# Up projection of a decoder layer: the halo kept in the first token half of four of seven parts; the two column halves of the first token tile of w_out no longer ordered one behind the other

## The chip, the cores and the metric

The kernel runs on one core of one Trainium2 chip. The metric is the device time of one execution in microseconds (us). Engines by the profile's names: PE is TensorE (matmuls; PEld its weight loads), DVE VectorE, ACT ScalarE, POOL GpSimd, SP SyncE, whose queue issues most DMAs.

## The reference

One layer over 16 meta tokens and 1024 tokens of width 1024. The part that matters here is its last third:

```python
mixed = jax.nn.sigmoid(g_attn) * y_attn + jax.nn.sigmoid(g_conv) * y_conv
h = layer_norm(DEEPNORM_ALPHA * h + mixed @ w_out, ln1_g, ln1_b)
up = causal_dwconv(h @ ffn_w_up, ffn_dw, ffn_dw_b)     # 3 taps, 2 x 2816 channels
u, g = jnp.split(up, 2, axis=-1)
f = (jax.nn.gelu(g, approximate=False) * u) @ ffn_w_down
return layer_norm(DEEPNORM_ALPHA * h + f, ln2_g, ln2_b)   # the meta tokens are dropped
```

The convolution has three taps and looks back, so each channel of a token needs the up projection of the two tokens before it too: the halo.

## The kernel before

All matrix products work on float32 split into a high and a low part, and add three products: high times high, high times low, low times high.

**Projection to `mixed` and w_out.** The last group of the projections (`ps_p`, L1173) is followed by `out_rows` (L1330 on), which multiplies `mixed` by w_out one tile of 128 tokens at a time, in the order 3, -1, 7, 2, 6, 0, 4, 1, 5. Tile -1 is the two tokens of the halo (the edge rows, L1358, matmuls of 32 rows). A tile has two column halves of 512; each is a PSUM buffer `ps_w` (three in turn under the tag `mm`) and 24 matmuls: eight blocks k of w_out rows, each with L340, L343 and L344 of `product`. Blocks 4 and 5 lie in RX and RW, 0 to 3 in OA, 6 and 7 in the two buffers `w`, and are split by a ScalarE cast (L300) and a VectorE subtraction (L303). `behind` gives `product` a matmul that its first one is to come after in program order; `after` puts such an order on two instructions without a semaphore. VectorE adds the residual (L1346; it is loaded from `h0d`), takes the statistics and normalizes (L1372); `turn` transposes the tile and ScalarE writes it with gain and offset to FA (L1395).

**Up projection.** It is one level of Strassen's scheme in Winograd's form: the tokens make two halves h, the 1024 inputs two halves kk, the output channels two halves, and seven products ("parts") of half size replace eight. The token side of the parts is `B11, B21, BT2, BT1, BT3, BT4, B22`: `bsub` forms the sums (`form_t2`, `form_t3`, `form_t4`) and `bsplit` splits each into `row(sub, q, 0)` and `row(sub, q, 1)`. Each half of 512 tokens is in turn cut into `sub` 0 (256 tokens, with the halo of two in front: 258 columns) and `sub` 1 (256). In `sub` 0 of each part the high operand has 260 columns: the low parts of the two halo columns, the high parts of the same two, and 256 more.

There are 22 chunks c of 128 + 128 output channels. In each, `prod` runs the parts in the order B11, B21, BT2, BT4, BT1, BT3, B22, and each part's `sub` 0 and then its `sub` 1, 12 matmuls each (L1597), into the PSUM tiles X (`px`), Z (`pz`), V4 (`pw`) and Y (`py`). In `sub` 0 the terms go by the kind of product (`j` in 0, 2, 1), since only two kinds hold the halo; in `sub` 1 they go by block k. Between the parts ScalarE copies X and Y out (L1609) and VectorE adds and subtracts them (L1605) to c11, c21 (first token half), c12 and c22 (second). `conv_ffn` first adds the two halo columns' low sums to their high ones (two activations of one column, L1521), then does the three taps. `w_ahead(9)` keeps the split weights of nine parts ready. Chunk 0 is run in two passes, `sub` 1 first.

**What sets the order.** A list scheduler with a timeline of its own orders each engine's instructions by `rank`, by dependences and by `after`; `line` pins VectorE's sums of the token side into one sequence. The down projection (L1742) follows.

Of the kernel before, what the change touches and what calls it, by code (L numbers as in the profile page):

```python
# [23 lines left out]
F = mybir.dt.float32  # L24
# [5 lines left out]
P = 128  # L30
# [83 lines left out]
def tile_hybrid_layer(  # L114
# [1118 lines left out]
            [(OC, OC_UP + i * 2048, 0) for i in range(4)] + [(RHC, x + R_DN, 0) for x in (4096, 2048, 6144)]]  # L1233
    B11, B21, BT2, BT1, BT3, BT4, B22 = range(7)

    def bsum(sub, q, hl):
        r = row(sub, q, hl)
        return r[:, :, 2:260] if sub == 0 and not hl else r

    def row(sub, q, hl):  # L1240
# [6 lines left out]
    def bmat(sub, q, j, k):  # L1247

        if sub:
            return row(1, q, j % 2)[:, k]  # L1250
        return row(0, q, j % 2)[:, k, 0:(260, 256, 260)[j]]

    lined, high = [], []
# [15 lines left out]

    def bsplit(sub, q, src, cs=slice(None)):  # L1270
        with rank(RK_SUMS):
            src = wide(src)[:, :, cs]
            hi = bsum(sub, q, 0)[:, :, cs]
            ins = nc.scalar.copy(hi, src)
            if (sub, q) in ((0, BT2), (0, BT4), (0, BT1), (0, BT3)):
                if high:
                    after(ins, high[-1])
                high.append(ins)
            n = src.shape[2]
            a = cs.start or 0  # L1280
            x = 2 if sub == 0 and a == 0 else 0
            a -= 2 if sub == 0 and a else 0
            lo = bsum(sub, q, 1)[:, :, a:a + n - x]
            line(nc.vector.tensor_tensor(lo, src[:, :, x:], f32(hi)[:, :, x:], OP.subtract))
            if x:
                line(nc.vector.tensor_tensor(row(0, q, 0)[:, :, 0:2], src[:, :, :2], f32(hi)[:, :, :2], OP.subtract))
# [28 lines left out]


    WO_ORDER = (4, 5, 0, 1, 2, 3, 6, 7)
    edge = const.tile([P, 2, KC, 2], F, name="edge")
    r_next, w_last = [1], []

    def out_rows(i, between=(), work=()):


        n, u = (P, 2 + i * P) if i >= 0 else (2, 0)
        if n == P:
            o = r_next[0] % 2 * 1024
            r_next[0] += 1
            whole = RT[:, o:o + 1024]
            load(whole, h0d[u:u + n, :])
        else:  # L1330
            whole = OB[:, 2048:3072]
        r = whole[:n]
        order = WO_ORDER if i != 5 else (0, 1, 2, 3, 6, 7, 4, 5)
        turned = None
        st = small.tile([P, 2, 6], F, name="st")
        pin = line if i in (0, 4, 1, 5) else lambda ins: ins
        for half in range(2):
            hs = slice(half * 512, half * 512 + 512)
            ps = pat.tile([P, 512], F, name="ps_w", tag="mm", bufs=3)
            if n == P:  # L1340
                behind = turned or (w_last[-1] if w_last else None)
                last = product(ps, [(mixed(i, k, 0), mixed(i, k, 1), wo[k][0][:, hs], wo[k][1][:, hs])
                                    for k in order], behind)
                w_last.append(last)
                with rank(RK_TURN):
                    pin(nc.vector.tensor_tensor(r[:, hs], ps, r[:, hs], OP.add))  # L1346
                    pin(nc.vector.bn_stats(st[:, half], r[:, hs]))
                turned = None
                if len(between) > half:
                    turned = turn(*between[half], behind=[last])  # L1350
                if half == 0:
                    for f, *x in work:
                        f(*x)
                continue

            for k in range(KC):
                o = k % 4 * 32
                last = nc.tensor.matmul(ps[o:o + 32], pair[:, 2 * k:2 * k + 32], wo_raw[k][:, hs], start=k < 4,  # L1358
                                        stop=k >= 4)
                after(last, w_last[-1])  # L1360
                w_last.append(last)
            nc.scalar.copy(whole[:, hs], ps)
        if n < P:
            for j, src in enumerate((h0d[0:2, :], whole[32:34], whole[64:66], whole[96:98])):
                q = FA[:2, j % 2 * 1024:j % 2 * 1024 + 1024]
                load(q, src)
                nc.vector.tensor_tensor(r, r, q, OP.add)
        with rank(RK_TURN):
            (mu, rs), = ln_stats([(r, n)], half_stats=st if n == P else None)
            for a in (512, 0) if i == 5 else (None,):  # L1370
                x = r if a is None else r[:, a:a + 512]
                ins = pin(nc.vector.tensor_scalar(x, x, mu, rs, OP.subtract, OP.mult))  # L1372
        if n == P:
            load(h1d[u - 2:u - 2 + P, :], r)
        return whole, n, ins

    def turn(i, r, n, ins, banks=None, behind=None, upper=False):
        with rank(RK_TURN):
            for j, k0 in enumerate((4, 0) if upper else (0, 4)):
                ps = banks[j] if banks else pat.tile([P, 512], F, name="ps_h", tag="s", bufs=2)  # L1380
                for k in range(4):
                    ins = nc.tensor.transpose(ps[:, k * P:(k + 1) * P], r[:, (k0 + k) * P:(k0 + k + 1) * P], ident)
                    if behind:
                        after(ins, behind[-1])
                        behind.append(ins)
                for k in range(k0, k0 + 4):
                    src = ps[:, (k - k0) * P:(k - k0) * P + n]
                    if n < P:
                        dst = edge[:, 0, k]
# [5 lines left out]
                    nc.scalar.activation(dst, src, AF.Identity, bias=b1col(k), scale=g1col(k))  # L1395
                    if i == 3:
                        nc.scalar.activation(edge[:, 1, k], src[:, P - 2:P], AF.Identity, bias=b1col(k), scale=g1col(k))
        return behind[-1] if behind else None


# [68 lines left out]
            w_ahead(n)  # L1469

    def edges():
        for h in range(2):
            with rank(RK_TURN):
                nc.vector.tensor_copy(FA[:, h * 2064:h * 2064 + 2064].rearrange("p (k n) -> p k n", n=258)[:, :, 0:2],
                                      edge[:, h])

    ahead = []
    work = {0: [(split_of, 1, B11), (split_of, 1, B21), (split_of, 1, B22)],
# [36 lines left out]
    c11, c21, u2 = (FA[:, 4128 + i * CU:4128 + (i + 1) * CU] for i in range(3))  # L1515
    c12, c22, u13 = (RT[:, i * CU:(i + 1) * CU] for i in range(3))

    def conv_ffn(cc, o):
        t = ftmp()
        for i in range(2):  # L1520
            nc.scalar.activation(cc[:, 2 + i:3 + i], cc[:, 2 + i:3 + i], AF.Identity, bias=cc[:, i:i + 1], scale=1.0)  # L1521
# [52 lines left out]
    for c in range(FC):  # L1574
        V4, X, Z, Y = (pup.tile([P, 1024], F, name=n, tag=n) for n in ("pw", "px", "pz", "py"))
        passes = ((1,), (0,)) if c == 0 else ((0, 1),)
        for subs in passes:
# [4 lines left out]
            def at(t):  # L1582
                return t[:, 252 + a:252 + b]

            def prod(q, bank, first):
# [4 lines left out]
                    ah, al = w_ready[next(w_next)]  # L1590
                for sub in subs:
                    terms = [(k, j) for k in range(4) for j in range(3)]
                    if sub == 0:
                        terms = [(k, j) for j in (0, 2, 1) for k in range(4)]
                    for i, (k, j) in enumerate(terms):
                        o = bank[:, 512:768] if sub else bank[:, (252, 256, 252)[j]:512]
                        ins = nc.tensor.matmul(o, (ah, ah, al)[j][:, k * P:(k + 1) * P], bmat(sub, q, j, k),  # L1597
                                               start=first and i == 0, stop=i == 11, skip_group_check=not first)
                        if i == 0 and last_mm:
                            after(ins, last_mm[-1])  # L1600
# [14 lines left out]
                sums_load(c - 1 if c <= FH else c - 2)  # L1615
            tt(c11[:, a:b], at(Z), u13[:, a:b], OP.add)
            prod(BT2, X, False)
            copy(u2[:, a:b], at(X))
            if not last:
                turn(5, *last_rows, (V4, Z), last_mm, True)  # L1620
                for q in (B11, B21):
# [11 lines left out]
            copy(c22[:, a:b], at(Y))  # L1633
            prod(BT3, X, False)
            copy(u13[:, a:b], at(X))
            ins = tt(c22[:, a:b], c22[:, a:b], u13[:, a:b], OP.add)
# [4 lines left out]
            tt(c12[:, a:b], at(Y), u2[:, a:b], OP.add)  # L1641
            if last:
                f1 = conv_ffn(c22, c)
                f_out(c, 0, g0, conv_ffn(c21, c))
                f_out(c, 1, gelu(conv_ffn(c12, FC + c)), f1)
    up_stack.close()


# [247 lines left out]
```

## Time and profile before

| | us |
|---|---|
| median of 3 runs (1251.36 to 1253.63) | 1251.79 |
| profiled execution | 1251.86 |
| its span | 1250.1 |
| TensorE busy in the span | 1236.5 |
| VectorE busy | 1079.4 |
| ScalarE busy | 627.6 |

The granted clock is 0.999. The span runs from the first profiled instruction to the last; the 1.8 us beside it are the start and end of the execution. Rows in order of time have the start, the length, the engine, the line, the operation, the tiles (written <- read) and the shape, then the count; a bracket has the idle time of the engine ahead of it and what ended that. Ends of matmuls are modelled and overlap, so the spacing of starts is what TensorE really takes.

### The profile page before, as it was taken

Reading aid. Unit: us, or ns where it says so; the run is one execution under the profiler, and the core shown is the slowest. Engines: PE = TensorE matmul, PEld = TensorE weight load, DVE = VectorE, ACT = ScalarE, POOL = GpSimd, SP = SyncE. Lnnn points to the kernel's source line nnn. Section 1 sums busy time; section 2 is a strip of 40 time slices with the busy share of each in tenths; the row PEclk is TensorE's granted clock in tenths of the full one; section 3 lists DMA queues with packets and bytes.
Section 4 is the critical chain, followed back from the end, with each engine's and each line's share of the span. In section 5 each row is a group of like instructions: output and inputs, shape, how many; then the busy total and the mean of one; then the engine's idle time right before and its main releaser. Section 6 shows DMA issues by size and latency. Waiting matters only on the chain.

```text
span 1250.1 us, 23200 instructions
## 1 busy us (share of the span) xinstructions
PE 1236.5 (99%) x9176; PEld 1172.2 (94%) x9176; DVE 1079.4 (86%) x1857; ACT 627.6 (50%) x1284; POOL 7.4 (1%) x8
## 2 busy tenths in 40 slices
PE   9999999999999999999999999999999999999997
PEld 8999999999999999788899999999999998888886
DVE  8989999999978677548899999998999976996697
ACT  8433255555474233344666566565565654545330
POOL 0000000001000000000000000000000000000000
PEclk9999999999999999999999999999999999999999
DMA  7393633432256563322145555454454567998812
GB/s 262 118 296 99 194 90 98 112 92 81 73 159 177 164 165 103 103 101 84 52 167 201 191 189 200 162 209 144 157 205 182 196 222 249 394 358 319 277 60 84
DMA packets 98695, 212.22 MB, mean 170 GB/s; under 512 B 11399, under 2 KB 38599, under 8 KB 98330
## 3 DMA queue, kind: packets, MB, share of 16 engines
q1 hardware_dynamic: 84422, 199.59, 47.6%
q10 hardware_dynamic: 14164, 11.15, 2.9%
q8 instruction: 72, 1.18, 0.4%
q14 instruction: 37, 0.30, 0.1%
HBM read 150.29 MB, written 62.70 MB: 170 GB/s over the span
## 4 chain that ended last, share of the span: by engine, by line
PE 91%; DVE 5%; DMA 2%; ACT 1%; issue 1%; SPq 0%; DVEq 0%; ACTq 0%
PE px L1597 13%; PE ps_x L1742 9%; PE py L1597 8%; PE ps_z L340 8%; PE ps_z L343 8%; PE ps_z L344 8%; PE ps_p L1173 7%; PE ps_z L1742 5%; PE pz L1597 4%; PE pw L1597 4%; PE ps_w L344 2%; PE ps_w L340 2%; PE ps_w L343 2%; PE ps_z L575 2%; PE ps_t L943 1%
## 5 line engine op out<-in xcount | busy, mean ns | idle before, releaser
L340 PE MATMUL ps_z<-RHO,w 128*128 128x256 f32 (+2 forms) x864 | 243.2, 281 | 0.0
L343 PE MATMUL ps_z<-RHO,w 128*128 128x256 f32 (+2 forms) x864 | 242.2, 280 | 0.0
L344 PE MATMUL ps_z<-RHC,w 128*128 128x256 f32 (+2 forms) x864 | 242.2, 280 | 0.0
L343 PEld LDWEIGHTS ps_z<-RHO,w 128*128 128x128 f32 x864 | 162.5, 188 | 0.5
L344 PEld LDWEIGHTS ps_z<-RHC,w 128*128 128x128 f32 x864 | 162.7, 188 | 0.2
L340 PEld LDWEIGHTS ps_z<-RHO,w 128*128 128x128 f32 x864 | 162.5, 188 | 0.1
L749 DVE SCALAR_TENSOR_TENSOR FA<-cin,cdw,FA 128x1026 f32<-128x1026 f32 x120 | 154.3, 1296 | 0.7
L300 ACT CAST w<-wr 128x1024 fp32r<-128x1024 f32 x37 | 38.8, 1048 | 61.7 <-PE ps_z L344 48.0
L1415 DVE TENSOR_TENSOR RHO<-wr,RHO 128x512 fp32r<-128x512 f32 x94 | 64.0, 684 | 3.7 <-ACT RHO L1414 3.5
L1414 ACT CAST RHO<-wr 128x512 fp32r<-128x512 f32 x94 | 56.9, 619 | 18.2 <-DVE wr L1432 9.3
L758 ACT ACTIVATE FA<-ps_z,colr 128x258 f32<-128x258 f32 (+1 forms) x64 | 30.1, 472 | 60.5 <-PE ps_z L344 52.8
L1432 DVE TENSOR_TENSOR wr<-wr 128x512 f32<-128x512 f32 x88 | 60.1, 683 | 0.1
L303 DVE TENSOR_TENSOR w<-wr,w 128x1024 fp32r<-128x1024 f32 x37 | 45.0, 1217 | 7.6 <-ACT w L300 7.4
L1173 PE MATMUL ps_p<-OC,w 128*128 128x256 f32 (+1 forms) x384 | 48.1, 278 | 0.0
L1173 PE MATMUL ps_p<-OA,w 128*128 128x256 f32 (+1 forms) x384 | 47.8, 278 | 0.0
L1173 PEld LDWEIGHTS ps_p<-OC,w 128*128 128x128 f32 x384 | 46.1, 188 | 0.1
L1609 ACT COPY FA<-px 128x516 f32<-128x516 f32 (+2 forms) x23 | 13.1, 570 | 65.7 <-PE px L1597 65.7
L1173 PEld LDWEIGHTS ps_p<-OA,w 128*128 128x128 f32 x384 | 45.9, 188 | 0.0
L1415 DVE TENSOR_TENSOR w<-wr,w 128x512 fp32r<-128x512 f32 x60 | 40.7, 684 | 4.9 <-ACT w L1414 4.8
L1597 PE MATMUL px<-OA,RHO 128*128 128x260 f32 x324 | 43.0, 281 | 0.0
L1597 PE MATMUL px<-OC,RHO 128*128 128x256 f32 x324 | 41.3, 277 | 0.8 <-DVE OB L1346 0.8
L1414 ACT CAST w<-wr 128x512 fp32r<-128x512 f32 x60 | 36.2, 619 | 8.9 <-DMA wr<-in_w_up_dram 4.7
(445 smaller groups left out, 3109.8 us busy)
## 6 DMA issues: line engine op xcount, KB each, us to landing
wr<-in_w_up_dram SPq DMA_DIRECT2D x44, 512.0 KB, 4.5
wr<-in_w_z_dram SPq DMA_DIRECT2D x29, 512.0 KB, 4.0
OB<-in_w_down_dram SPq DMA_DIRECT2D x24, 512.0 KB, 4.7
fd<-FA SPq DMA_DIRECT2D x44, 256.0 KB, 2.4
FA<-sd SPq DMA_DIRECT2D x15, 512.0 KB, 9.2
qt<-qd SPq DMA_DIRECT2D x28, 256.0 KB, 4.1
OB<-td SPq DMA_DIRECT2D x14, 512.0 KB, 9.3
sgd<-FA ACTq DMA_DIRECT2D x48, 128.0 KB, 2.7
```

What stands on the lines that cost most here:

```text
L300: ins = nc.scalar.copy(hi, raw)
L303: return nc.vector.tensor_tensor(lo, raw, f32(hi), OP.subtract)
L340: ins = nc.tensor.matmul(ps, al, bh, start=i == 0, stop=False)
L343: nc.tensor.matmul(ps, ah, bh, start=False, stop=False)
L344: last = nc.tensor.matmul(ps, ah, bl, start=False, stop=i == n - 1)
L749: nc.vector.scalar_tensor_tensor(acc[c], cin[:, j:j + U], wc, acc[c], OP.mult, OP.add)
L1173: nc.tensor.matmul(ps[:, :b - a], x, rhs(k, hl, a, b), start=k + j == 0, stop=k == 3 and j == 2)
L1414: nc.scalar.copy(hi, src)
L1415: ins = nc.vector.tensor_tensor(lo, src, f32(hi), OP.subtract)
L1432: ins = nc.vector.tensor_tensor(*x)
L1597: ins = nc.tensor.matmul(o, (ah, ah, al)[j][:, k * P:(k + 1) * P], bmat(sub, q, j, k), start=first and i == 0, stop=i == 11, skip_group_ch ...
L1742: nc.tensor.matmul(banks[i], l[:, ts], r[:, ws], start=first and a and x + k == 0, stop=z and x == len(ops) - 1 and k == 2, skip_group_che ...
```

## The change

It has two independent sides.

**Halo.** `edges()` writes the halo of the second token half's inputs differently: the first token half's own halo again in the lower four blocks of the inputs, and zeros in the upper four. By the formulas of the sums the halo columns of BT2, BT1 and B22 are then zero, and B11, B21, BT3 and BT4 alone carry it. For the three others `bsplit` splits 256 columns, the matmuls of `sub` 0 have 256 columns and the term order of `sub` 1. The halo of c22 and c12 isn't computed but copied: it is the last two columns of c21 and c11 (`before`). The evacuations that need no halo start two or four columns later (`m`). The second copy of the edge rows, made by eight activations of two columns in `turn` of tile 3, goes.

**w_out.** `behind` is given at the start of tile 7 alone (18 entries in `w_last`: two halves and 16 edge matmuls), where before each half came behind the matmul before it. The edge matmuls come behind the last two entries, so behind both halves of tile 3.

```diff
+    HALO = (B11, B21, BT3, BT4)
     def bsum(sub, q, hl):
         r = row(sub, q, hl)
+        if sub == 0 and not hl and q not in HALO:
+            t, o, back = B_AT[0][q]
+            o += back * 1024
+            return t[:, o:o + 1024].rearrange("p (k n) -> p k n", k=4)
         return r[:, :, 2:260] if sub == 0 and not hl else r
...
+        if q not in HALO:
+            return (row(0, q, 1) if j == 1 else bsum(0, q, 0))[:, k]
         return row(0, q, j % 2)[:, k, 0:(260, 256, 260)[j]]
...
-            src = wide(src)[:, :, cs]
+            whole = sub == 0 and q not in HALO
+            src = wide(src)[:, :, slice(2, None) if whole else cs]
...
-            x = 2 if sub == 0 and a == 0 else 0
+            x = 2 if sub == 0 and a == 0 and not whole else 0
...
-                behind = turned or (w_last[-1] if w_last else None)
+                behind = turned or (w_last[-1] if len(w_last) == 18 else None)
...
-                after(last, w_last[-1])
+                for ins in w_last[-2:]:
+                    after(last, ins)
...
-                    if i == 3:
-                        nc.scalar.activation(edge[:, 1, k], src[:, P - 2:P], AF.Identity, bias=b1col(k), scale=g1col(k))
...
     def edges():
-        for h in range(2):
-            with rank(RK_TURN):
-                nc.vector.tensor_copy(FA[:, h * 2064:h * 2064 + 2064].rearrange("p (k n) -> p k n", n=258)[:, :, 0:2],
-                                      edge[:, h])
+        with rank(RK_TURN):
+            halo = FA[:, 0:2 * 2064].rearrange("p (k n) -> p k n", n=258)[:, :, 0:2]
+            nc.vector.tensor_copy(halo[:, 0:KC], edge)
+            nc.vector.tensor_copy(halo[:, KC:KC + 4], edge[:, 0:4])
+            nc.vector.memset(halo[:, KC + 4:], 0.0)
...
-    def conv_ffn(cc, o):
+    def conv_ffn(cc, o, before=None):
         t = ftmp()
-        for i in range(2):
-            nc.scalar.activation(cc[:, 2 + i:3 + i], cc[:, 2 + i:3 + i], AF.Identity, bias=cc[:, i:i + 1], scale=1.0)
+        if before is not None:
+            nc.scalar.copy(cc[:, 2:4], before[:, HW:CU])
+        else:
+            for i in range(2):
+                nc.scalar.activation(cc[:, 2 + i:3 + i], cc[:, 2 + i:3 + i], AF.Identity, bias=cc[:, i:i + 1],
+                                     scale=1.0)
...
-                    if sub == 0:
+                    if sub == 0 and q in HALO:
                         terms = [(k, j) for j in (0, 2, 1) for k in range(4)]
...
-                        o = bank[:, 512:768] if sub else bank[:, (252, 256, 252)[j]:512]
+                        o = bank[:, 512:768] if sub else bank[:, (252 if q in HALO and j != 1 else 256):512]
...
-            copy(u2[:, a:b], at(X))
+            copy(u2[:, m:b], at(X, m))
...
-                f1 = conv_ffn(c22, c)
+                f1 = conv_ffn(c22, c, c21)
                 f_out(c, 0, g0, conv_ffn(c21, c))
-                f_out(c, 1, gelu(conv_ffn(c12, FC + c)), f1)
+                f_out(c, 1, gelu(conv_ffn(c12, FC + c, c11)), f1)
```

How the instructions move, at three places. First TensorE at the first tile of w_out, before: `ps_w_6384` is the tile's half 0, `ps_w_6411` its half 1, `w_6371` and `w_6376` hold blocks 6 and 7.

```order
L343 MATMUL ps_w_6384<-OA_5087,RHC_79 128x512
L1173 MATMUL ps_p_6325<-OC_5083,w_6231 128x256 x12
L1173 MATMUL ps_p_6344<-OC_5083,w_6231 128x256 x12
L344 MATMUL ps_w_6384<-OA_5087,RHC_79 128x512
L340 MATMUL ps_w_6384<-w_6371,RHC_79 128x512
L343 MATMUL ps_w_6384<-w_6371,RHC_79 128x512
L344 MATMUL ps_w_6384<-w_6371,RHC_79 128x512
L340 MATMUL ps_w_6384<-w_6376,RHC_79 128x512
L343 MATMUL ps_w_6384<-w_6376,RHC_79 128x512
L344 MATMUL ps_w_6384<-w_6376,RHC_79 128x512
L340 MATMUL ps_w_6411<-RX_5274,RHC_79 128x512
```

Half 0 is finished with block 7 before half 1 begins; 17 matmuls of the tile stand ahead of the 24 of `ps_p`. The same engine and tile after the change, from its last matmuls into the edge rows (`ps_w_6448`, `ps_w_6458`):

```order
L344 MATMUL ps_w_6411<-w_6371,RHC_79 128x512
L340 MATMUL ps_w_6384<-w_6376,RHC_79 128x512
L343 MATMUL ps_w_6384<-w_6376,RHC_79 128x512
L340 MATMUL ps_w_6411<-w_6376,RHC_79 128x512
L343 MATMUL ps_w_6411<-w_6376,RHC_79 128x512
L344 MATMUL ps_w_6384<-w_6376,RHC_79 128x512
L344 MATMUL ps_w_6411<-w_6376,RHC_79 128x512
L1367 MATMUL ps_w_6448<-FA_78,pair_5279 32x512 x5
```

Block 7 now comes last in both halves, and its low part (L344) behind 46 of the tile's 48 matmuls; 22 of them stand ahead of the 24 of `ps_p`.

Then TensorE in a chunk of the up projection, parts BT2, BT4 and BT1 before (`sub` 0 in two rows, `sub` 1 in one):

```order
L1597 MATMUL px<-OA,RHO 128x260 x8
L1597 MATMUL px<-OA,RHO 128x256 x4
L1597 MATMUL px<-OC,RHO 128x256 x12
L1597 MATMUL pw<-OA,RHO 128x260 x8
L1597 MATMUL pw<-OA,RHO 128x256 x4
L1597 MATMUL pw<-RHC,RHO 128x256 x12
L1597 MATMUL py<-OA,RHO 128x260 x8
L1597 MATMUL py<-OA,RHO 128x256 x4
L1597 MATMUL py<-OC,RHO 128x256 x12
```

And after:

```order
L1612 MATMUL px<-OA,RHO 128x256 x12
L1612 MATMUL px<-OC,RHO 128x256 x12
L1612 MATMUL pw<-OA,RHO 128x260 x8
L1612 MATMUL pw<-OA,RHO 128x256 x4
L1612 MATMUL pw<-RHC,RHO 128x256 x12
L1612 MATMUL py<-OA,RHO 128x256 x12
L1612 MATMUL py<-OC,RHO 128x256 x12
```

BT2 and BT1 are 12 matmuls of 256 columns in either `sub`; the number and the place of the groups are the same.

Last ScalarE from one copy of `px` to the next in the up projection (`wr` is a raw weight, `FA` c11, c21 or a temporary, `OB` c12, c22 or an evacuation), before:

```order
L1609 COPY OB<-px 128x516
L1414 CAST w<-wr 128x512
L1521 ACTIVATE OB<-OB 128x1 x2
L1523 ACTIVATE FA<-OB,coll 128x512
L1521 ACTIVATE FA<-FA 128x1 x2
L1523 ACTIVATE FA<-FA,coll 128x512
L1414 CAST RHO<-wr 128x512
L1521 ACTIVATE OB<-OB 128x1 x2
L1609 COPY OB<-px 128x516
```

And after:

```order
L1624 COPY OB<-px 128x516
L1422 CAST w<-wr 128x512
L1422 CAST RHO<-wr 128x512
L1536 ACTIVATE FA<-OB,coll 128x512
L1530 COPY OB<-FA 128x2
L1533 ACTIVATE FA<-FA 128x1 x2
L1536 ACTIVATE FA<-FA,coll 128x512
L1624 COPY OB<-px 128x516
```

The halo copy (L1530) stands where c22's two activations stood, a row later, and c12's are gone from here: its copy stands earlier in the chunk.

More of the change, by code (lines that the diff above doesn't have):

```diff
@@ L1317, in tile_hybrid_layer @@
     WO_ORDER = (4, 5, 0, 1, 2, 3, 6, 7)
-    edge = const.tile([P, 2, KC, 2], F, name="edge")
+    edge = const.tile([P, 2, KC, 2], F, name="edge")[:, 0]
     r_next, w_last = [1], []
@@ L1388, in turn @@
                     if n < P:
-                        dst = edge[:, 0, k]
+                        dst = edge[:, k]
                     else:
@@ L1632, in tile_hybrid_layer @@
             prod(BT1, Y, True)
-            copy(c22[:, a:b], at(Y))
+            copy(c22[:, m:b], at(Y, m))
             prod(BT3, X, False)
             copy(u13[:, a:b], at(X))
-            ins = tt(c22[:, a:b], c22[:, a:b], u13[:, a:b], OP.add)
+            ins = tt(c22[:, m:b], c22[:, m:b], u13[:, m:b], OP.add)
             if last and c not in (0, FH + 1):
@@ L1640, in tile_hybrid_layer @@
             prod(B22, Y, False)
-            tt(c12[:, a:b], at(Y), u2[:, a:b], OP.add)
+            tt(c12[:, m:b], at(Y, m), u2[:, m:b], OP.add)
             if last:
-                f1 = conv_ffn(c22, c)
+                f1 = conv_ffn(c22, c, c21)
                 f_out(c, 0, g0, conv_ffn(c21, c))
-                f_out(c, 1, gelu(conv_ffn(c12, FC + c)), f1)
+                f_out(c, 1, gelu(conv_ffn(c12, FC + c, c11)), f1)
     up_stack.close()
```

3 lines of the change are left out of this document (2 added, 1 removed).

## The prediction

> **What bounds the kernel now.** I read the page first (busy shares, then the chain that ended last), then TensorE's waits, then TensorE's rows in order of time at the places that the change touches.
>
> ```profile
> span 1250.1 us, 23200 instructions
> PE 1236.5 (99%) x9176; PEld 1172.2 (94%) x9176; DVE 1079.4 (86%) x1857; ACT 627.6 (50%) x1284; POOL 7.4 (1%) x8
> PE 91%; DVE 5%; DMA 2%; ACT 1%; issue 1%; SPq 0%; DVEq 0%; ACTq 0%
> ```
>
> TensorE (PE) is busy 99% of the span and is 91% of the chain that ended last. What its waits by partner add up to is small:
>
> ```profile
> PE pw L1597 <- ACT FA L1395: 1.2, 1, 1.2
> PE px L1597 <- DVE OB L1346: 0.8, 1, 0.8
> PE ps_w L344 <- DVE w L303: 0.5, 1, 0.5
> ...
> PE ps_w L340 <- ACT w L300: 0.2, 1, 0.2
> PE ps_z L1742 <- DVE RHC L1692: 0.2, 1, 0.2
> ```
>
> So time is won in two ways only: matmuls that follow each other more closely, or one of these few waits removed. The up projection (L1597) has no wait here but those at its very start; the two on ps_w are the tile of w_out that the change reorders.
>
> One chunk of the up projection, by the start times of its groups of 12 matmuls (the numbers are start and length; I use differences of starts, since ends are modelled):
>
> ```profile
> 642.41 1.59 PE L1597 MATMUL px<-RHC,w 128*128 128x260 f32 x12
> ...
> 647.98 1.59 PE L1597 MATMUL px<-OA,w 128*128 128x260 f32 x12
> 649.41 1.52 PE L1597 MATMUL px<-OC,w 128*128 128x256 f32 x12
> 650.77 1.58 PE L1597 MATMUL pw<-OA,w 128*128 128x260 f32 x12
> ...
> 653.54 1.58 PE L1597 MATMUL py<-OA,RHO 128*128 128x260 f32 x12
> 654.96 1.52 PE L1597 MATMUL py<-OC,RHO 128*128 128x256 f32 x12
> ...
> 659.10 1.59 PE L1597 MATMUL py<-RX,RHO 128*128 128x260 f32 x12
> 660.53 1.52 PE L1597 MATMUL py<-RHC,RHO 128*128 128x256 f32 x12
> 661.89 0.88 PE L1597 MATMUL px<-RHC,RHO 128*128 128x260 f32 x6
> ```
>
> A group named 128x260 is a first token half (eight matmuls of 260 columns, four of 256); a group of 128x256 is the second half with the same weights. The reader is to see that BT2 takes 649.41 - 647.98 = 1.43 us in the first half and 650.77 - 649.41 = 1.36 in the second, BT1 1.42 in the first half, B22 1.43 against 1.36.
>
> **The change, part by part.**
>
> *1. Three parts lose their halo (BT2, BT1, B22).* Eight of 12 matmuls go from 260 to 256 columns and the terms go in the order of the second half. Price: the chunk runs from 642.41 to 661.89, 19.48 us; its seven second halves are 7 x 1.36 = 9.52, so the seven first halves take 9.96, 1.423 each, 0.063 more than 1.36. Three parts save 0.19 us per chunk, and 22 chunks 4.15 us, all on TensorE without a wait, so all on the path. The bounds: a column costs 1.36 us / 12 / 256 = 0.443 ns, and 4 columns x 8 x 3 x 22 = 2,112 columns by that are 0.94 us; the other end is 0.07 for each of 66 groups, 4.6 us. I take 4.15: the nearest row is the same weights on 256 columns right behind, and 32 columns by column price explain 14 of the 63 ns only, so the rest hangs on the odd width (or on the term order, which also becomes the second half's). The Trainium skill, "TensorE: Matmul & The Clock Gate", section "Back-to-back issue gap", gives an isolated gap of N / 2.4 + 2.5 ns; by it the four columns are 1.7 ns and this part would come to 0.9 us. The row of 1.43 against 1.36 differs from that rule, and the sum goes by the row.
>
> *2. First tile of w_out (token tile 3): its column halves may be interleaved.* Before, half 0 runs into the split of the last two row blocks of w_out and half 1 waits behind it:
>
> ```profile
> 496.80 0.40 PE L340 MATMUL ps_w<-RX,RHC 128*128 128x512 f32 x1
> ...
> 500.68 2.99 PE L1173 MATMUL ps_p<-OC,w 128*128 128x256 f32 x24
> 503.51 0.40 PE L344 MATMUL ps_w<-OA,RHC 128*128 128x512 f32 x1
> ...
> 506.45 0.39 PE L340 MATMUL ps_w<-RX,RHC 128*128 128x512 f32 x1
> ...
> 511.69 0.39 PE L344 MATMUL ps_w<-w,RHC 128*128 128x512 f32 x1
> 512.01 1.48 PE L1358 MATMUL ps_w<-FA,pair 128*32 128x512 f32 x9
> ...
> 513.75 1.45 PE L1358 MATMUL ps_w<-FA,pair 128*32 128x512 f32 x9
> ```
>
> Half 1 is undisturbed: 511.69 - 506.45 = 5.24 us for 23 steps, 0.228 each. The tile's 48 matmuls at 0.228 and the 24 of ps_p (503.51 - 500.68 = 2.83) make 13.8 us, but 496.80 to 512.01 is 15.2: 1.4 us are lost, to the two waits above (0.2 and 0.5) and the slow starts behind them. In the new order 46 of the 48 are placed ahead of the first low part of the last row block, so TensorE would get there at about 510.1. That block's split is late by only five matmuls (ps_p and its merges move behind five more), 1.1 us, while before it was ready shortly ahead of 506.45. The edge matmuls take no weights of it, and its high part, due three matmuls earlier, is ready before the low one. I take 1.3 of the 1.4 as won.
>
> What comes late next: the edge rows' second half (513.75) takes the PSUM buffer of the tile's half 0, which VectorE must have read; that read waits for a load of the residual.
>
> ```profile
> 504.49 2.26 SPq L125 DMA_DIRECT2D OB<-h0d  x2
> 505.98 0.42 DVE L1192 SCALAR_TENSOR_TENSOR RHC<-OB,RHC 128x256 fp32r<-128x256 f32 x1
> 510.59 0.69 DVE L1346 TENSOR_TENSOR OB<-ps_w,OB 128x512 f32<-128x512 f32 x1 [4.20 <-DMA OB<-h0d]
> ```
>
> The second load of SyncE's row waits for the last merge (L1192, done at 506.40); with the merge 1.1 us later the read starts at 510.59 + 1.14 = 511.73 and ends at 512.42. The edge rows would start at 510.6 and their second half 1.74 later, at 512.35. That costs 0.1 to 0.3 with the restart; I take 0.2. Net 1.1. Bounds: 1.4 if the load comes in time, and nothing, or a few tenths below, if it lands 1.3 us later than this. SyncE's other rows there stay in order, but for a store of h1d that goes behind two loads of w_up.
>
> Is the 1.1 us kept? At the end of w_out VectorE is ready just ahead:
>
> ```profile
> 597.36 0.69 DVE L1290 TENSOR_TENSOR FA<-OB,FA 128x520 f32<-128x520 f32 x1
> 599.38 0.69 DVE L1346 TENSOR_TENSOR OB<-ps_w,OB 128x512 f32<-128x512 f32 x1 [1.32 <-PE ps_w L344]
> 600.12 1.68 PE L1597 MATMUL px<-OC,RHO 128*128 128x256 f32 x12 [0.78 <-DVE OB L1346]
> ```
>
> VectorE idles 1.32 us ahead of 599.38, the read that frees TensorE. Even if none of its work moved up, it covers 1.1. If that cover went, the price is at most the 1.1.
>
> *3. Small work.* Gone: eight edge activations, 88 of 176 one-column ones, which become 44 copies of two columns, and three little subtractions. Added: a copy and a memset on VectorE in edges().
>
> ```profile
> L1395 ACT ACTIVATE edge<-ps_h,colr 128x2 f32<-128x2 f32 x8 | 2.2, 352 | 3.5 <-PE ps_h L1382 3.5
> L1521 ACT ACTIVATE OB<-OB 128x1 f32<-128x1 f32 x82 | 19.6, 287 | 13.7 <-DVE OB L1605 13.7
> 613.84 0.15 DVE L1286 TENSOR_TENSOR OA<-OB,OA 128x8 fp32r<-128x8 f32 x1
> ```
>
> ScalarE loses 8 x 0.35 + 44 x 0.29 = 15.6 us if a copy costs what one of these did, VectorE 3 x 0.15 and gains about 0.3. I cost all of it at nothing: TensorE, busy throughout, covers it. A halo copy adds a dependence: c22's halo now comes from c21, the same channels' first token half (c12's from c11), so ScalarE waits for one subtraction more in its queue, with a weight cast and the next evacuation of px behind it.
>
> ```profile
> L1605 DVE TENSOR_TENSOR FA<-OB,pw 128x516 f32<-128x516 f32 x20 | 13.7, 684 | 0.0
> 644.30 0.48 ACT L1521 ACTIVATE OB<-OB 128x1 f32<-128x1 f32 x2 [0.24 <-DVE OB L1605]
> 645.45 0.59 ACT L1609 COPY OB<-px 128x516 f32<-128x516 f32 x1 [0.67 <-PE px L1597]
> ```
>
> That subtraction is 0.68 us, ScalarE idles 0.67 ahead of the copy at 645.45, and the copy (done 646.04) is wanted by BT2 at 647.98: 1.9 us to spare. Cover gone, it costs what exceeds 1.9 + 0.67.
>
> The down projection moves up as a whole: its one wait (ps_z, 0.2) hangs on the last store of f, which comes from the same chunk.
>
> Sum: 4.15 + 1.1 = 5.25. The profiled execution took 1251.86 (span 1250.1 and 1.8 around it), the median of the runs is 1251.79; 1251.86 - 5.25 gives 1246.6, 0.42% less.
>
> **Rivals.**
>
> *Columns only.* The 63 ns come from something that stays (say the place of a first half in its PSUM bank), and the change saves 0.94. For: even the four matmuls of 256 columns in a first half are part of its slower 1.42. Against: second halves run at 1.36 right after. Time: 1251.86 - 0.94 - 1.1 = 1249.8. The Trainium skill's gap rule named above leads to this same result.
>
> *w_out gives nothing.* The load of the residual lands later, or VectorE's 1.32 is used up: 1251.86 - 4.15 = 1247.7. For: only 0.2 us lie between the freed cover and my gain at the end of w_out.
>
> *VectorE takes over.*
>
> ```profile
> 622.93:642.41 19.48, 19.48 (x171) 19.48 (x169) 18.87 (x33) 15.54 (x34) 0.00 (x0) 1.00 0.40 136
> ```
>
> In the first full chunk (columns: length, PE, PEld, VectorE, ScalarE) VectorE works 18.87 of 19.48 us; the chunk is to become 19.29. Its reordered queue need lose only 0.4 us per chunk to bind. If half of the first term goes: 1251.86 - 2.1 - 1.1 = 1248.7. Against: this is the fullest row, TensorE never waits for it, and weights are split nine ahead.
>
> *Slower: the halo copy holds up px.* If the new wait makes ScalarE's copy of px late in each chunk, TensorE waits at BT2. It decides against the change once the lateness exceeds the 1.9 us by 5.25 / 22 = 0.24, so from about 2.1 us; at 2.5 us late the loss is 22 x 0.6 = 13.2 against 5.25, 1259.8. The wait that I see is 0.68 behind 0.67 of idle time.
>
> **How the numbers follow.** My sum 0.67; w_out nothing 0.13; columns only 0.09; VectorE 0.07; slower 0.04. A difference of 0.2% (2.5 us) is about what a measurement of this kernel can tell from none, so faster means below 1249.3: the sum, w_out nothing and VectorE, 0.87. Columns only is within it, 0.09. The range reaches from both upper bounds, 4.6 + 1.4 = 6.0 and 0.4 for the spread between the lower two runs (1251.36 and 1251.79), 1245.4, to just past the VectorE case, 1249.0.
>
> **What will show it.** Right: TensorE's groups of px<-OA, py<-OA and py<-RX as 256 x12 with 1.36 between starts; chunks of 19.29 instead of 19.48; matmuls of 260 columns down from 1,232 to 704; no wait on w L300 or L303 and a small one of the edge matmuls on the residual's read. Wrong: first halves still at 1.40 or more though 256 wide, a new row of TensorE waiting for ScalarE's px copy or VectorE inside the chunks, or a wait at 598 to 600 longer than 0.8.

## The result, and the profile after

The changed kernel takes 1249.69 us (median of 15 runs, 1248.47 to 1252.14) against 1252.48 for the kernel before in the same session (1251.36 to 1253.88): a ratio of 0.9976 [0.9969, 0.9983], 2.8 us less where 5.25 were forecast; the median lies 0.7 us above the forecast range of 1245.4 to 1249.0. Its profiled execution took 1251.82 us and is among the longest of the 15. Two profiled executions below ran at a fraction of the speed, after_again's from 815 us on and the first of by_kind_near (2512.69 us) throughout; nothing is read from those stretches, and the ratios leave both out.

Its page, and TensorE's waits:

```profile
span 1250.0 us, 23157 instructions
PE 1234.0 (99%) x9176; PEld 1170.0 (94%) x9176; DVE 1077.5 (86%) x1855; ACT 613.7 (49%) x1232; POOL 7.4 (1%) x8
```

```profile
PE ps_h L518 <- DVE xn L497: 2.1, 1, 2.1
...
PE ps_h L1392 <- issue: 1.2, 1, 1.2
PE pw L1612 <- ACT FA L1405: 1.2, 1, 1.2
PE px L1612 <- DVE OB L1355: 0.8, 1, 0.8
```

The two waits on w_out's split rows are gone, as forecast. Two rows are new: 1.2 us at the transposes (L1392), and 2.1 us at the kernel's start, where no instruction was changed; w_out begins 1.73 us later in this profile than before (498.53 against 496.80), which takes back in this one execution nearly all that the rest of it wins.

A chunk of the up projection after (compare the differences of starts with those of before):

```profile
682.70 1.59 PE L1612 MATMUL px<-RHC,RHO 128*128 128x260 f32 x12
...
688.27 1.56 PE L1612 MATMUL px<-OA,RHO 128*128 128x256 f32 x12
689.68 1.53 PE L1612 MATMUL px<-OC,RHO 128*128 128x256 f32 x12
691.04 1.58 PE L1612 MATMUL pw<-OA,RHO 128*128 128x260 f32 x12
...
693.81 1.52 PE L1612 MATMUL py<-OA,RHO 128*128 128x256 f32 x12
695.17 1.52 PE L1612 MATMUL py<-OC,RHO 128*128 128x256 f32 x12
...
702.09 0.28 PE L1612 MATMUL px<-RHC,w 128*128 128x260 f32 x1
```

BT1's first half takes 695.17 - 693.81 = 1.36 us as forecast, BT2's 1.41 (medians over 21 chunks: BT1 1.360, BT2 and B22 1.403, and 1.363 in the second halves behind these). The chunk is 19.39 us, not 19.29: it saves 0.094 us, 2.1 in 22 chunks, in place of 4.15.

w_out after: the tile's two halves run through to 512.38, and then VectorE and TensorE at tile 7:

```profile
498.53 0.40 PE L340 MATMUL ps_w<-RX,RHC 128*128 128x512 f32 x1
...
512.38 1.48 PE L1367 MATMUL ps_w<-FA,pair 128*32 128x512 f32 x9
...
514.12 1.45 PE L1367 MATMUL ps_w<-FA,pair 128*32 128x512 f32 x9
```

```profile
527.53 1.22 DVE L1377 TENSOR_TENSOR OB<-OB,FA 2x1024 f32<-2x1024 f32 x1 [2.74 <-DMA FA<-OB]
...
533.74 0.81 DVE L1382 TENSOR_SCALAR OB<-OB,mv,sd 128x1024 f32<-128x1024 f32 x1
```

```profile
533.08 0.39 PE L344 MATMUL ps_w<-w,RHC 128*128 128x512 f32 x1
534.66 1.06 PE L1392 MATMUL ps_h<-coll,OB 128*128 128x128 f32 x8 [1.19 <-issue]
...
601.87 0.86 PE L1612 MATMUL px<-OC,RHO 128*128 128x256 f32 x5 [0.78 <-DVE OB L1355]
```

From w_out's first matmul (498.53) to the edge rows are 13.85 us against 15.21 before: 1.36 are won there. But VectorE stands 2.74 us behind a load of the edge rows' partial sums (last of the four adds of L1377). Tile 7's statistics and normalization are queued behind that add, and TensorE, now there earlier, waits 1.19 us for them. From w_out's first matmul to the up projection's first it is 103.34 us, before 103.32.

### The profile page after: what moved, and what is told of

Its sections match the earlier page's. It is cut to its first block, busy times and chain, and to the rows that moved or that the text cites. A ratio compares the mean times of both kernels' runs of the same rounds, so it can differ in the third digit from the quotient of the medians.

```text
span 1250.0 us, 23157 instructions
## 1 busy us (share of the span) xinstructions
PE 1234.0 (99%) x9176; PEld 1170.0 (94%) x9176; DVE 1077.5 (86%) x1855; ACT 613.7 (49%) x1232; POOL 7.4 (1%) x8
## 4 chain that ended last, share of the span: by engine, by line
PE 94%; DVE 3%; DMA 1%; ACT 1%; issue 1%; SPq 0%; DVEq 0%
PE px L1612 15%; PE py L1612 9%; PE ps_x L1757 9%; PE ps_z L340 8%; PE ps_z L343 8%; PE ps_z L344 8%; PE ps_p L1173 7%; PE ps_z L1757 5%; PE pz L1612 5%; PE pw L1612 5%; PE ps_w L340 2%; PE ps_w L344 2%; PE ps_w L343 2%; PE ps_z L575 2%; PE ps_t L943 1%; PE ps_s L919 1%
## 5 line engine op out<-in xcount | busy, mean ns | idle before, releaser
L344 PE MATMUL ps_z<-RHC,w 128*128 128x256 f32 (+2 forms) x864 | 242.2, 280 | 0.0
L344 PEld LDWEIGHTS ps_z<-RHC,w 128*128 128x128 f32 x864 | 162.7, 188 | 0.2
L1624 ACT COPY FA<-px 128x512 f32<-128x512 f32 (+1 forms) x23 | 13.1, 569 | 71.2 <-PE px L1612 71.2
L1612 PE MATMUL px<-OA,RHO 128*128 128x256 f32 (+1 forms) x324 | 42.7, 281 | 0.0
L1536 ACT ACTIVATE FA<-OB,coll 128x512 f32<-128x512 f32 x44 | 35.8, 815 | 14.0 <-DVE OB L1620 14.0
```

The source lines that it names most:

```text
L344: last = nc.tensor.matmul(ps, ah, bl, start=False, stop=i == n - 1)
```

## The experiments

Stage times below are differences of starts in one profiled execution of each kernel: "w_out" from its first matmul to the up projection's first, groups as medians over 21 chunks. Ratios are to the kernel before on the same chip.

### The two sides apart: up_only, wout_only

up_only has the lines of `behind` and of the edge matmuls as before; wout_only is the kernel before with these two edits alone.

> The halo side of the change alone; w_out keeps its order of before. If the two sides are independent: BT1's first half 1.360 us, BT2's and B22's 1.40, chunks of 19.39 as in the changed kernel, w_out with the waits of before (w L300 0.2, w L303 0.5) and no idle time at the transposes of tile 7. Time: about 2.1 us less than before from the 22 chunks, so 0.9983 of before. If the w_out side was worth the 1.1 us of my sum, this one loses 1.1 against the changed kernel; if what it wins is lost again at tile 7, as the trace after suggests, it is within 0.3 us of it.

> The w_out side of the change alone; the up projection as before. Theory (the gain is given back): the stage from the first matmul of w_out to the first of the up projection is shorter by 0.3 us at most, with about 1.2 us of TensorE idle at the transposes of tile 7 in place of the waits on w; time within 0.3 us of before. Rival (the idle time at tile 7 came with the other side of the change, the edge rows' second copy that is gone): the stage is shorter by 1.1 us and the time 1.1 less.

up_only: 0.9991 [0.9982, 1.0], so 1.1 us where 2.1 were expected, with 2.1 still in the interval; groups as in the changed kernel, w_out 103.30. In one chunk TensorE waited for ScalarE's copy of px, which the kernel before does not do; ahead of the copy ScalarE's queue has weight casts, the first of which stood 2.67 us behind a load of w_up:

```profile
PE px L1611 <- ACT OB L1623: 0.7, 1, 0.7
```

```profile
743.68 1.14 ACT L1421 CAST w<-wr 128x512 fp32r<-128x512 f32 x2 [2.67 <-DMA wr<-in_w_up_dram]
```

wout_only: 1.0001 [0.9991, 1.001]; w_out 104.11, 0.8 longer than before, with 1.55 us of idle time at tile 7's transposes. The w_out side can give all back by itself; the halo side is not needed for the idle time.

### Is the give-back fixed? after_again, after_third, edge_on_pool, edge_late

> The changed kernel unaltered, for a second profiled execution. Theory (the idle 1.2 us at tile 7's transposes hangs on when the last load of the edge rows lands, which differs from execution to execution): w_out's length differs from the 103.34 us of the first, between 102.1 (load early) and 104, with the groups of the up projection as before (BT2 and B22 1.403, BT1 1.360). Rival (the idle time is fixed by the order of this kernel): 103.3 again.

> The changed kernel unaltered, for a third profile: w_out between 101.9 and 104 us by the landing of the edge rows' last load, chunks of 19.39, and a wait at the start (L518) of 0 to 2.5 us if it is chance, 1.3 or more if it comes with the new halo.

The same program's second profiled execution, up to the end of w_out (its other executions put the ratio at 0.9984 [0.9972, 0.9995]):

```profile
526.69 1.22 DVE L1377 TENSOR_TENSOR OB<-OB,FA 2x1024 f32<-2x1024 f32 x1 [1.20 <-DMA FA<-OB]
...
532.91 0.81 DVE L1382 TENSOR_SCALAR OB<-OB,mv,sd 128x1024 f32<-128x1024 f32 x1
```

```profile
534.02 1.04 PE L1392 MATMUL ps_h<-coll,OB 128*128 128x128 f32 x8
```

The last add starts 27.45 us behind w_out's first matmul (499.24), not 29.00, no idle time follows, and w_out takes 101.92. The third (after_third) has the load late again, w_out 103.37. Over the twelve profiles with the new order and unmoved edge adds w_out took 101.9 to 104.1 us, 102.8 in the mean, and follows the start of the last add behind its first matmul: 27.5 to 27.8 us with 101.9 to 102.1, 28.8 to 29.1 with 103.1 to 103.4, 29.8 with 104.1. So the 1.1 us of my sum come and go with the landing of one load.

edge_on_pool (`nc.gpsimd.tensor_tensor(r, r, q, OP.add)` for the four adds):

> The changed kernel with the four adds of the edge rows' partial sums (2 x 1024, each behind a load) on GpSimd instead of VectorE. If they held up VectorE's queue ahead of tile 7's normalization: the idle 1.2 us of TensorE at the transposes of tile 7 is gone and w_out takes 102.2 to 102.4 us instead of 103.34, 1.0 us less in all. Rival (the transposes wait for the statistics of tile 7 themselves, or for ScalarE): the idle time stays.

```profile
522.75 7.30 POOL L1377 TENSOR_TENSOR OB<-OB,FA 2x1024 f32<-2x1024 f32 x3 [3.83 <-issue]
```

```profile
530.08 1.27 DVE L262 BATCH_NORM_STATS2 st<-OB 2x6 f32<-2x512 f32 x2 [1.70 <-POOL OB L1377]
```

A miss: GpSimd takes 2.4 us for an add where VectorE takes 1.2, and the edge rows' statistics (L262), still in VectorE's queue ahead of tile 7, wait for it. The idle time grew to 2.8, w_out to 105.29, the time to 1.0007 [0.9998, 1.0016]. What holds tile 7 is VectorE's queue, not the adds as such. edge_late, which also has lo_moved's layout (below), changes the order alone:

```diff
-            two = (i, *out_rows(i))          # edge rows: all four adds, statistics
+            finish = out_rows(i)             # matmuls only
...
         if i == 7:
-            ahead.append(two)
+            norm = [rows[2]]                 # adds 3 and 4: after(add, norm[0])
+            two = (-1, *finish())
+        if i == 2:
+            ahead.append(two)                # transposes one tile later
```

> lo_moved, and the last two adds of the edge rows behind tile 7's normalization on VectorE, their transposes one token tile later. If those adds and their loads hold up tile 7: w_out takes 102.1 us whatever the load does, no idle time of TensorE at its transposes; with chunks of 19.29 the whole is 4.1 + 1.2 = 5.3 us below before, about 0.9958 of it. Rival (the edge rows are then late for the halo or for their own transposes): a wait of a microsecond or more appears at a later tile.

```profile
529.03 0.81 DVE L1385 TENSOR_SCALAR OB<-OB,mv,sd 128x1024 f32<-128x1024 f32 x1
529.75 2.45 DVE L1378 TENSOR_TENSOR OB<-OB,FA 2x1024 f32<-2x1024 f32 x2
```

Tile 7 is normalized ahead of the late adds; w_out takes 101.95 us without idle time, and 102.10 and 101.95 in the two kernels below that have the same order. With lo_moved's slower groups the whole is 0.9977 [0.9968, 0.9986].

### Why BT2 and B22 stayed slow: same_phase, bt1_apart, lo_moved

My theory was the distance between high and low parts. In the changed kernel BT1's two parts lie 1024 floats apart, BT2's and B22's 1056. same_phase and bt1_apart move high parts, in `bsum`:

```diff
-            o += back * 1024
+            o += back * 1024 + (0 if back else 32)     # same_phase: BT2, B22 now 1024
+            o += back * (1024 + 32)                    # bt1_apart: BT1 now 1056
```

> The changed kernel with the high parts of BT2 and B22 placed 1024 floats ahead of their low parts (as BT1's are) and not 1056. Theory (a matmul whose moving operand starts at another place within a short stretch of a partition's memory than the one before it costs about 5 ns, since 1056 floats are 128 bytes off a multiple of 256): both first halves fall from 1.40 to 1.360, the chunk from 19.39 to 19.30, 2.0 us in all. Rival (it hangs on which buffer or which end of a row the operand lies in): they stay at 1.40, time unchanged.

> The changed kernel with BT1's high part 32 floats later, so that high and low are 1056 floats apart as in BT2 and B22, and nothing else. Theory 1: BT1's first half goes from 1.360 to 1.40, with its second half 3 ns slower, 22 x 0.046 = 1.0 us more. Rival (BT1 was fast because of its place among the parts or its buffer): 1.360 stays.

BT2 in same_phase, then BT1 in bt1_apart:

```profile
686.02 1.52 PE L1612 MATMUL px<-OA,RHO 128*128 128x256 f32 x12
687.38 1.52 PE L1612 MATMUL px<-OC,RHO 128*128 128x256 f32 x12
```

```profile
693.21 1.56 PE L1612 MATMUL py<-OA,RHO 128*128 128x256 f32 x12
694.62 1.53 PE L1612 MATMUL py<-OC,RHO 128*128 128x256 f32 x12
```

Both as the theory had it: 1.360 for BT2 and B22 (chunk 19.294, the very length forecast; 0.997 [0.9957, 0.9983]), and 1.403 for BT1 (0.9987 [0.9976, 0.9998]). lo_moved makes the same distance of 1024 by moving the low parts (`hi = HP if sub == 0 and q in HALO else 256` in `row`):

> The distance of BT2's and B22's operands made 1024 floats from the other end: the low parts move 32 floats ahead, the high parts stay where the changed kernel has them. Theory 1 (the distance of high and low counts): 1.360 in both, chunks of 19.29, 2.0 us less than the changed kernel. Rival (the place of the high parts itself, 32 and 128 bytes behind a multiple of 256, is what is slow): 1.40 stays.

```profile
687.39 1.57 PE L1612 MATMUL px<-OA,RHO 128*128 128x256 f32 x12
688.81 1.53 PE L1612 MATMUL px<-OC,RHO 128*128 128x256 f32 x12
```

Here the theory fell: 1.413, slower still (0.9982 [0.9973, 0.9992]). What the fast cases share is the place: the start of the moving operand in its partition, in bytes beyond a multiple of 256 as the built program has it (a buffer's start and the offset in it). Weights start at 96 throughout the up projection. All second halves and BT1 after start at 32; the high parts of BT2 and B22 at 160, in lo_moved the low parts too; in same_phase all at 32.

### Place, order or what came before: by_kind, by_kind_near, halo_by_k

by_kind runs the first halves without halo in the term order of before (`if sub == 0:` for the order alone); by_kind_near adds same_phase's edit, halo_by_k is same_phase with the halo parts by block k.

> The changed kernel with the term order of before (all of j 0, then 2, then 1) in the first halves of the three parts without halo; the places stay. High and low operands then follow each other once in 12 matmuls, not eight times. Theory of the start places: BT2 and B22 fall from 1.40 to about 1.365, BT1 stays at 1.36; about 1.7 us less in all. Rival (columns or place of the buffer): 1.40 stays. Rival (the term order itself is what costs in first halves): all three rise to about 1.41.

> by_kind and same_phase in one: high and low parts of BT2 and B22 1024 floats apart as in BT1, and the first halves without halo run by kind of product. by_kind had 1.41 in both halves of BT2, BT4 (second half), BT1 and B22, same_phase 1.360 in all. Theory 1 (only the distance of the operands counts; BT1 was slow in by_kind because it inherits the rhythm of BT2 ahead of it): 1.360 again, time as same_phase, about 0.997 of before. Theory 2 (the term order alone makes a group slow, and the groups behind it keep its rhythm): 1.41 in the same groups, time as by_kind, about 1.0025 of before.

> by_kind_near once more, whose first profile was of an execution at half the speed. Theory 1: BT2, BT1 and B22 1.360 in both halves, chunks of 19.29. Theory 2: 1.41 as in by_kind.

> same_phase with the first halves of the four halo parts run by block k too (260, 256, 260 columns in turn); their places stay. Theory 2 (term order): B11, B21, BT3 and BT4 fall from 1.427 and 1.413 to about 1.374 (12 at 113.3 ns and 8 x 4 columns more), 4 x 0.05 x 22 = 4.4 us less than same_phase. Theory 1 (distances: their high rows are 264 floats apart, so that high and low of a block differ by 32 floats and more): they stay at 1.41 or above, no gain.

BT2 in by_kind, first and second half:

```profile
686.32 1.58 PE L1612 MATMUL px<-OA,RHO 128*128 128x256 f32 x12
687.73 1.58 PE L1612 MATMUL px<-OC,RHO 128*128 128x256 f32 x12
689.14 1.59 PE L1612 MATMUL pw<-OA,RHO 128*128 128x260 f32 x12
```

by_kind is slower than before, 1.0026 [1.0017, 1.0035]: 1.41 in BT2, BT1 and B22, which is what its rival of the term order had said, but also in the second halves of these and of BT4, which nothing touched and no theory had foreseen. Its matmuls follow each other at 117.7 ns in place of 113.3, one steady spacing. by_kind_near has the same order with all at 32 (ratio 0.9968 [0.9957, 0.9978]): 1.360 in all of them and 19.29 per chunk in its second profile, by_kind_near2, here BT2:

```profile
686.08 1.52 PE L1612 MATMUL px<-OA,RHO 128*128 128x256 f32 x12
687.44 1.52 PE L1612 MATMUL px<-OC,RHO 128*128 128x256 f32 x12
688.80 1.58 PE L1612 MATMUL pw<-OA,RHO 128*128 128x260 f32 x12
```

So the order by itself does not slow them. In halo_by_k the halo parts gained nothing (1.437, 1.425); behind BT4, BT1's two halves, whose instructions and places are same_phase's, run at 1.413:

```profile
691.30 1.58 PE L1610 MATMUL py<-OA,RHO 128*128 128x256 f32 x12
692.72 1.58 PE L1610 MATMUL py<-OC,RHO 128*128 128x256 f32 x12
694.13 1.61 PE L1610 MATMUL px<-OA,RHO 128*128 128x260 f32 x12
```

A group can keep the spacing of the group ahead of it. Time 0.9997 [0.9987, 1.0006].

### More places: places, ring_shift, back_all, stride272

> The changed kernel with all of BT2's and BT1's first half starting at 96 bytes beyond a multiple of 256 and B22's at 224 (32 and 160 were seen before: 113.3 and 117.7 ns per matmul). Theory 3 (only some places are slow): a constant spacing of its own for 96 and for 224, either 113.3 or about 117.7; most likely 96 fast and 224 slow, if 128 bytes of difference are what matters. Theory 1 (only changes of place matter): 113.3 at both, after the first matmul.

BT2 (at 96) and B22 (at 224):

```profile
687.55 1.58 PE L1613 MATMUL px<-OA,RHO 128*128 128x256 f32 x12
688.97 1.54 PE L1613 MATMUL px<-OC,RHO 128*128 128x256 f32 x12
...
698.71 1.59 PE L1613 MATMUL py<-RX,w 128*128 128x256 f32 x12
700.13 1.55 PE L1613 MATMUL py<-RHC,w 128*128 128x256 f32 x12
```

Both slow, 1.421 and 1.428, without a change of place inside the group: at 96 the last four of the twelve matmuls are 120.0 ns apart. Time 1.0005 [0.9996, 1.0015]. That 96 would be fast was wrong; of four places, 32 alone was, with weights at 96.

ring_shift moves two of the ten places of split weights to 224 (`RHO[:, 6240 + ...]` for 6272), on same_phase:

> same_phase with two of the ten places that split weights cycle through moved by 128 bytes, so that some groups load weights that start at 224 bytes beyond a multiple of 256 and the others at 96, with moving operands unmoved at 32. Theory 3a (what counts is the start of the moving operand against the start of the weights, modulo 256 bytes): second halves and the first halves of BT2, BT1 and B22 take 1.41 us in the groups with moved weights and 1.360 in the others. Theory 3b (the start of the moving operand alone): 1.360 everywhere.

B11's second half, with weights at 224:

```profile
682.73 1.57 PE L1612 MATMUL px<-OC,RHO 128*128 128x256 f32 x12
684.14 1.59 PE L1612 MATMUL pz<-RHO 128*128 128x260 f32 x12
```

With weights at 224 the second halves behind a halo group rise to 1.41 (18 of 18; with weights at 96 none), though their moving operands stay at 32. So theory 3b falls. But BT2, BT1 and B22 with weights at 224 stay at 1.360 behind a group of 1.360 (10 of 10) and take 1.41 behind one of 1.41 (2 of 2), which 3a in its plain form doesn't allow either: at this place a group keeps the spacing that it finds. Place of weights, place of operand and the spacing of the group ahead all count.

back_all lays out every part to begin at 32, in edge_late's order; stride272 spaces the halo rows 272 floats apart in place of 264, and puts the high rows of the four halo parts ahead of their low ones. The edit shown is back_all's:

```diff
-    B_AT = [[(RHC, 16, 0), (RHO, 4096 + 16, 0)] + [(OA, 8 + i * 2080, i % 2) for i in range(4)] + [(RX, 32, 0)],
+    B_AT = [[(RHC, 48, 1), (RHO, 4096 + 48, 1), (OA, 40, 0), (OA, 2088, 0), (OA, 4136, 1), (OA, 6248, 1), (RX, 64, 0)],
```

> edge_late with every part's operands placed so that they begin at 32: the three parts without halo whole, the four halo parts with their high rows at 32, 64, 96 and 128 (as BT4's were) in place of 160, 192, 224 and 0. Theory 3: BT2, BT1 and B22 1.360, B11, B21 and BT3 as BT4, 1.413 in place of 1.427; chunks 7 x 1.360 + 3 x 1.360 + 4 x 1.413 = 19.25, 0.23 less than before, 5.0 us in all; with w_out at 102 us, 1.3 less, about 6.3 us below before: 0.995.

> back_all with the high rows of the halo parts 272 floats apart, so that they start at 32, 96, 160 and 224. Theory 3 with 32 the only fast place: no better than back_all's 1.413. If the size of the step between rows counts (64 bytes for 32): 1.42 to 1.43. If 96 is fast too and 160 and 224 slow: about 1.40, 1.0 us below back_all.

```profile
679.68 1.58 PE L1621 MATMUL px<-RHC,RHO 128*128 128x260 f32 x12
681.09 1.52 PE L1621 MATMUL px<-OC,RHO 128*128 128x256 f32 x12
...
698.93 1.58 PE L1621 MATMUL px<-RHC,w 128*128 128x260 f32 x12
```

back_all: 698.93 - 679.68 = 19.25 us, as expected, w_out 102.10, and 1248.47 us, 0.9969 [0.9958, 0.9979]; its ratio is below the changed kernel's 0.9976, but the intervals overlap. The whole is a miss: 6.3 us less than before were expected and 4.0 measured. In its profiled execution (1246.51 us) it is 5.35; there 0.9 us go in two chunks in which ScalarE's copy of px came late. The rest stays open. stride272, BT2:

```profile
687.52 1.58 PE L1621 MATMUL px<-OA,RHO 128*128 128x256 f32 x12
688.94 1.58 PE L1621 MATMUL px<-OC,RHO 128*128 128x256 f32 x12
```

Every group of 256, all at 32, is at 1.413, and the time 1.0054 [1.004, 1.0067]: one layout of the halo rows locks the whole chunk into the slower spacing.

### The start: before_again

> The kernel before, unaltered, for a second profiled execution. In the first its wait at the start (L518, for the first tiles of the input) was under 0.1 us, against 1.3 to 2.5 in most profiles of kernels with the changed halo and 0.2 and 0.5 in two. If that wait is chance: anything from 0 to 2.5 us here. If it comes with the old halo: under 0.6 again. The rest as in the first: w_out 103.3 us, chunks of 19.48.

0.4 us, w_out 103.29, chunks of 19.48. The profiles with the old halo have 0.06, 0.4 and 0.5 us at L518; 14 of 16 with the new one 1.3 to 2.5 (after_third 1.4), with the same instructions there. But the length of the wait is not what the start loses. In halo_by_k TensorE comes to L518 at 7.97 us and waits 1.5, in the kernel before it comes at 9.34 and waits 0.06, and in both the next matmul starts at 9.73; w_out begins at 496.71 and 496.80. With the new halo w_out begins at 496.7 to 499.2 us, 497.6 in the mean, with the old at 496.8 to 497.3. That the 0.6 us between the means belong to the change is not shown; I found no cause, and it stays open.

## Why the prediction was right or wrong

- **Bound.** Right: TensorE is busy 99% and what it saves shows.
- **Term 1, 4.15 us: mis-sized, 2.06 measured.** The step that failed is "the nearest row is the same weights on 256 columns right behind". That row has the columns and the term order, but its operands all start at 32; BT2 and B22 took over a layout made for 264-float rows, with the high parts at 160. With these at 32 (same_phase) the group falls to 1.360 and the chunk to 19.294, the length that the prediction gave. The 2.06 lie within the bounds of 0.94 and 4.6. That the rest of the 63 ns "hangs on the odd width (or on the term order, which also becomes the second half's)" left out this third difference between the rows.
- **Term 2, 1.1 us: right where it was argued, unreliable as a whole.** 1.36 us are won at the first tile, no wait on the residual's read grew into a loss, and with edge_late's order the stage keeps 1.2 to 1.4. The step that failed is "What comes late next", which stopped at the edge matmuls: the next one late was tile 7's normalization, behind the edge rows' adds in VectorE's queue. I had not looked up these two rows of the profile before:

```profile
525.78 1.22 DVE L1367 TENSOR_TENSOR OB<-OB,FA 2x1024 f32<-2x1024 f32 x1 [1.36 <-DMA FA<-OB]
```

```profile
532.93 1.04 PE L1382 MATMUL ps_h<-coll,OB 128*128 128x128 f32 x8
```

From the late add's start to the transposes are 7.15 us, and 7.13 after, where TensorE waited for just this chain (534.66 - 527.53): already before it ended in the moment when TensorE came, 1.36 us late by its load, and there was no cover for anything won upstream. In the mean of twelve profiles 0.5 us remain.
- **Term 3, nothing:** nearly right. The halo copy makes no wait in each chunk. Single waits of 0.2 to 0.7 us for the copy of px appear in some profiles with the new halo and in none of the three with the old; the 21 chunks are longer by them and what follows them, from 0.3 us in the changed kernel's first profile to 1.4 in up_only. That is far from the 2.1 us of lateness per chunk at which that rival decides, and in the two longest of these waits (up_only, after_third) ScalarE had idled 2.67 and 2.32 us for a load of w_up, not for the halo copy.
- **Rivals.** "Columns only" was wrong in its mechanism: BT1 fell by 54 ns, where its columns are worth 14. The estimate of 1249.8 by the Trainium skill's "TensorE: Matmul & The Clock Gate", section "Back-to-back issue gap", lies beside the median of 1249.69 by luck: matmuls of equal columns were 113.3, 117.7 and 120.0 ns apart here, which a rule by columns alone doesn't give. "w_out gives nothing" had the result of the first and third execution, not of the second, and neither of its causes: it was neither the residual's load nor the cover at the end of w_out. In the chunks VectorE never became the bound.
- **Sum.** 2.06 + 0.5 = 2.6 us by the stages, 2.8 measured. What the single waits cost, and the later start of w_out if it belongs to the change (0.6 us in the mean), have to come off the first number: from its first matmul to the down projection's first the up projection was 1.82 us shorter in this profile (430.07 against 431.89). The spread of the runs (3.7 us) doesn't decide that.

## What to carry to other kernels

A price read from a neighbouring row holds only if everything that differs is named, and where an operand starts in memory is part of it: when an operand shrinks, lay it out anew. When a wait is removed from TensorE, follow the in-order queues of its feeders to the next tile and the one after; work that was ready just in time has become late. A gain that hangs on the landing of one load should be looked at in several profiled executions.

## What the hardware showed that I had not expected

- Matmuls of 128x256 that follow each other with the same shape have several spacings: 113.3 ns (operand at 32, weights at 96), 117.7 (operand at 160), 120.0 (operand at 96, in the last four of twelve). Over 22 chunks the place of two operands was worth 2.1 us (same_phase against the changed kernel), more than the 0.94 of the columns saved.
- The spacing can be inherited: the same instructions at the same places ran at 113.3 or at 117.7 by what came ahead of them, in whole chunks (stride272). What makes a slow run fall back (in lo_moved within three matmuls of the second half, in by_kind not in the second halves of BT2, BT4, BT1 and B22) stays open.
- GpSimd took 2.4 us for an add of 2x1024 that VectorE did in 1.2.
